# Narrow half first in some weight units, early parts for the fourth sums, a smaller first load and three more warm-up matmuls

## Chip, cores and metric

The kernel runs on one core of a Trainium2 chip. The metric is the device time of one execution in microseconds (us), the median of several runs. Engines are TensorE (PE; PEld is its weight load), VectorE (DVE), ScalarE (ACT), GpSimd (POOL) and SyncE (SP, which only issues DMAs here).

## What is computed

One layer of a streaming encoder on x of 512 tokens by 2048 channels, all in float32:

```
hn    = rmsnorm(x, norm_g)
proj  = hn @ w_in           # 3 branches x (q, k, v, gate) x 512, 4 forget logits, 3 x 2048 merge gates
ya    = forgetting_attention(...)   # branch A, 4 heads of 128
yb    = chunked_relpos_attention(...)  # branch B
yc    = stick_breaking_attention(...)  # branch C
ys    = stack(ya, yb, yc) * silu(gate)
merged = sum over branches of sigmoid(merge gates) * (ys @ w_up)
out   = x + merged @ w_out
```

q and k of branches A and B are normed per head. The three big products (with w_in, w_up and w_out) are nearly all of TensorE's work.

## The kernel before

**Operands in two parts.** Every float32 operand of a big product is split into a high part (rounded by a ScalarE copy, line 245) and a low part (the rest, a VectorE subtraction, line 249); a product is high x high, high x low and low x high. For weights the tiles are wh and wl. For the moving side a Parts tile holds high and low of 256 tokens side by side, so one matmul of 512 columns does high weights times both parts (wide), and one of 256 columns does low weights times the high part (narrow).

**Fewer products.** Two neighbouring column tiles of 128 are computed together in a PairTask by seven products instead of eight, over halves of the channels and of the tokens (the Strassen scheme). Products 1, 2, 3 and 5 read quarters of x (or of merged, the m tiles) or sums of them, products 6 and 7 read the tiles t23 (m23), product 4 reads t4 (m4): the "fourth sums". Each product is one weight unit of eight 128x128 tiles, a Pair: eight wide matmuls, then eight narrow ones (`mms_of`, lines 646 to 680). In most tasks the order is 1, 2, 6, 5, 7, 3, 4, and products 6, 7, 4 and 3 add onto the PSUM bank of an earlier one (`onto`). A `late` task and the very last product are all narrow (`single`): 24 matmuls of 256 columns. VectorE makes the weight sums for products 6 and 3 (`sums`, lines 625 to 639); those for 7 and 5 come by a second, adding DMA.

**Stages.** First a quad of four column tiles over the 16 channel tiles, in nine spans as x arrives (`first_quad`); then one late task and 45 other tasks on x, with the attention's small matmuls put between them; then the up-projection, where each of 16 output tiles has two units of 18 wide matmuls (three branches), whose results are weighted by gates reloaded from DRAM and added (`taken`); then eight tasks with w_out on the merged tiles, the first of them late.

**The merged tiles.** When output tiles k and k+8 are there, `merged_b` (lines 1399 to 1430) splits one of them, makes the sums of the two, and waits for room: `up_half` and `up_done` are set when the up-projection's last unit begins and when the first unit of the output projection begins, and free operand tiles (xps). The parts of product 4's sums, m4, are made last, in `late_t4` (lines 1432 to 1441): the unsplit sums wait in working tiles mu, two to a tile.

**What sets the order.** A planner, `Flow`, runs the whole program as tasks with costs per operation and due times, and writes the orders of TensorE, ScalarE and VectorE by hand; a task's spawn gives its slack, which sets its due time. `stream` (line 1529) walks the units on TensorE; `prep` splits a unit's weights, spawned two units ahead, with three buffers each for wh and wl. Working tiles of 512 columns (t2) are 20 in number, one of which holds constants (onef, zerof, nu_f) for good; raw weights have six (raws). Loads go on SP's queue, the first weights on ScalarE's, adding DMAs on POOL's.

**The start.** One DMA, `begin`, brings the first tile of x and all small constants (lines 292 to 299). VectorE copies two of them (gq, w2) ahead of its first work on x. POOL fills constants; `onef` is the third. Sixteen matmuls of constants (WARM, line 1543) run first on TensorE.

Of the kernel before, what the change touches and what calls it, by code (L numbers as in the profile page):

```python
# [15 lines left out]
P = 128  # L16
# [46 lines left out]
class Flow:  # L63
# [98 lines left out]
def hybrid_kernel(  # L162
# [2 lines left out]
    xT: bass.AP,  # L165
    xn: bass.AP,
    begin: bass.AP,
    w_one: bass.AP,
    w_two: bass.AP,
    w_col: bass.AP,  # L170
# [28 lines left out]
    def t2(s, dt=F32):  # L199
        return tp.tile([P, S], dt, tag="t2", name=nm(s))  # L200
# [14 lines left out]
    def blk(i):  # L215
        return slice(i * P, (i + 1) * P)
# [46 lines left out]
    def mm(ps, w, x, start=False, stop=False, more=False):  # L263
        nc.tensor.matmul(ps, w, x, start=start, stop=stop, skip_group_check=more)  # L264
# [30 lines left out]
    gn = small_in[:, 0:KT]  # L295
    gqk = small_in[:, KT:KT + 4]
    bfc = small_in[:, KT + 4:KT + 5]
    bg = small_in[:, KT + 5:KT + 5 + NB * DT]
    wf = small_in[:, KT + 5 + NB * DT:].rearrange("p (k h) -> p k h", h=NH)

    epsc = cp.tile([P, 1], F32, name="epsc")
    nc.gpsimd.memset(epsc, EPS)
    nhepsc = cp.tile([P, 1], F32, name="nhepsc")
    nc.gpsimd.memset(nhepsc, -0.5 * EPS)
    tmpc = t2("tmpc")
    onef, zerof, nu_f = tmpc[:, blk(0)], tmpc[:, blk(1)], tmpc[:, blk(2)]
    nc.gpsimd.memset(onef, 1.0)
# [20 lines left out]
    nc.gpsimd.memset(zeroc, 0.0)  # L328

    gq = cp.tile([P, 4], F32, name="gq")  # L330
    nc.vector.tensor_copy(gq, gqk)
    for c in (0, 2):
        nc.vector.tensor_scalar_mul(gq[:, c:c + 1], gqk[:, c:c + 1], SCALE)  # L333

    w2 = cp.tile([P, KT * NH + 32], F32, name="w2")
    nc.vector.tensor_copy(w2[:, :KT * NH].rearrange("p (k h) -> p k h", k=KT), wf)
    nc.vector.tensor_copy(w2[:, KT * NH:], zerof[:, :32])
    t2s.free.pop()


# [11 lines left out]
    class Unit:  # L352


        def __init__(self, mms, after=None, shape=(UK, P), srcs=()):
            self.shape, self.mms, self.after, self.srcs = list(shape), mms, after, srcs
            self.ready_hi, self.ready, self.there, self.raw = Event(), Event(), Event(), None

        def source_there(self):
            return self.there  # L360
# [208 lines left out]
    class Pair(Unit):  # L569


        def __init__(self, task, i):
            super().__init__(task.mms_of(i), task.after_of(i))
            self.task, self.p = task, task.order[i]

        def source_there(self):
            if self is self.task.units[0]:
                spawn(self.task.sums(), 3.0)
            return self.task.there[self.p]

        def source(self):
# [6 lines left out]
    class PairTask:  # L588
# [57 lines left out]
        def mms_of(self, i):  # L646
            p = self.order[i]
            bank = (0, 1, 2, 0, 0, 1, 2)[i] if self.late else {2: 1, 5: 2, 3: 2}.get(p, 0)
            onto = None if self.late else {6: 1, 7: 6, 4: 7, 3: 5}.get(p)
            more = onto is not None  # L650
            single = self.late or self.plain_end and p == 4
            self.bank = getattr(self, "bank", {})
            self.bank[p] = bank

            def go(u):
                if more:
# [6 lines left out]
                for j in range(UK):  # L663
                    yield lambda: self.ops[p](j) is not None
                    r, _, ev = self.ops[p](j)
                    yield ev
                    if single:
                        yield PE, mm_us(HS)
                        mm(self.ps[p][:, LH], u.hi[:, j, :], r[:, 0, :], j == 0 and not more, more=more)
                    else:  # L670
                        yield PE, mm_us(S)
                        mm(two(self.ps[p]), u.hi[:, j, :], r, j == 0 and not more, more=more)
                    if single:
                        yield PE, mm_us(HS)
                        mm(self.ps[p][:, LH], u.hi[:, j, :], r[:, 1, :], more=more)
                yield u.ready
                for j in range(UK):
                    yield PE, mm_us(HS)
                    mm(self.ps[p][:, LH], u.lo[:, j, :], self.ops[p](j)[1], stop=j == UK - 1, more=more)
            return go  # L680

        def after_of(self, i):
# [701 lines left out]

        return [Unit(mms(i), shape=(6, P), srcs=[w_up[d, i]]) for i in range(2)]

    m1, m2, m23, m4 = [None] * UK, [None] * UK, [None] * UK, [None] * (UK // 2)
    m4_ev = [Event() for _ in range(UK // 2)]
    kept_m, m1_ev, mus, up_half, up_done = {}, [Event() for _ in range(UK)], {}, Event(), Event()

    def merged_a(k, a):

# [6 lines left out]
    def merged_b(k, b):  # L1399
        a = kept_m[k]  # L1400
        yield m1_ev[k]
        yield t2s, 1
        t = t2("mt")
        if k % 2 == 0:
            yield t2s, 1
            mus[k // 2] = t2("mu")
        u = mus[k // 2][:, RH if k % 2 else LH]
# [24 lines left out]
    def late_t4(k, u, due):  # L1432
        if k % 2 == 0:
            yield xps, 1
            m4[k // 2] = Parts("m4")
            set_(m4_ev[k // 2])
        yield m4_ev[k // 2]
        h, lo, ev = m4[k // 2].half(k % 2)
        yield from split(h, lo, u, HS, ev, (due + 14.0,))
        if k % 2:  # L1440
            give(t2s)

    for k in range(UK):
        for d in (k, k + UK):
# [4 lines left out]
    at(len(units), freed(xps, 6, up_done))  # L1449


    mops = strassen_ops(m1, m2, m23, m4)

    def out_pair(e):
        evs = [Event(), Event()]
# [42 lines left out]
    def loads():  # L1498
        def x(kt):
            if kt == 0:  # L1500
                xraw[kt], x_in[kt].t = x_begin, landing(0.0, 256)
                return
            yield t2s, 1
            xraw[kt] = t2("x")
            x_in[kt].t = fetch(xraw[kt], xT[kt], 0.0, 256).t

        def n(i):
            yield t2s, 1
            t = t2("xn")
            n_in[i].t = fetch(t, xn[i // NQ, i % NQ], 0.0, 256).t  # L1510
            spawn(square_x(i, t), 10.0)

        todo = list(range(NQ * QB))
        for i, sp in enumerate(spans):

            for kt in [kt for sp in spans[i:i + (2 if i > 2 else 1)] for kt in range(*sp)]:
                if xraw[kt] is None:
                    yield from x(kt)
            yield from load_unit(units[i])
            if i >= N_FROM:  # L1520
                for _ in range(N_PER):
                    if todo:
                        yield from n(todo.pop(0))
        for i in todo:
            yield from n(i)
        for u in units[len(spans):]:
            yield from load_unit(u)

    def stream():
        for i, u in enumerate(units):  # L1530
            cur[0] = i
            for g in side.pop(i, ()):
                spawn(g(), 5.0, flow.fin)
# [3 lines left out]
            yield u.ready_hi  # L1537
            yield from u.mms(u)
            if u.after is not None:
                spawn(u.after(), 0.0, flow.fin)  # L1540
# [16 lines left out]

NT = 20
KEPT = 1
WARM = 16  # L1560
SPANS = [(0, 1), (1, 2)] + [(k + h, k + h + 2) for k in range(0, UK, 2) for h in (0, UK)][1:]
N_ONE = 2
NX = 28
# [56 lines left out]
```

## Time and profile before

| | us |
|---|---|
| median of three timed runs | 1327.93 |
| the three runs | 1326.29, 1327.93, 1328.51 |
| the profiled execution's own time | 1328.65 |
| its span, first to last instruction | 1326.9 |
| TensorE busy in the span | 1320.2 |
| VectorE busy | 1134.7 |
| ScalarE busy | 805.9 |

The span is what the trace shows; the execution's own time has the little before and after it. In a timeline row stand the start and the time taken in us, the engine, the line, the operation, out<-in by the program's names, the shape, the count of instructions merged in the row, and in brackets the idle time before it with what ended it. Matmuls overlap: a row's time taken holds the tail of its last one, so the pace is read from start to start. A wide matmul shows as 128x512, a narrow one as 128x256; a row with wh uses the high weights, one with wl the low ones.

### The profile page before, as it was taken

The numbers are of one execution on the slowest core, as the hardware profiler recorded it, in microseconds if no ns is written. First come the engines' busy times: TensorE is split into PE (matmuls) and PEld (weight loads), VectorE is DVE, ScalarE is ACT, GpSimd is POOL, SyncE is SP. The second block draws the span as 40 slices with busy tenths as digits, with TensorE's granted clock in tenths as the row PEclk, the third lists the DMA queues.
The fourth block names the chain that finished last, engine by engine and source line by source line (L and its number), as shares of the span: only waits on it lengthen the run. The fifth ranks groups of instructions, "written<-read, shape, count | busy, mean of one in ns | idle before, by whom it ended". The sixth has DMA issues, their size and how long they took to land.

```text
span 1326.9 us, 20238 instructions
## 1 busy us (share of the span) xinstructions
PE 1320.2 (99%) x7506; PEld 1150.5 (87%) x7506; DVE 1134.7 (86%) x1676; ACT 805.9 (61%) x1280; POOL 94.9 (7%) x120
## 2 busy tenths in 40 slices
PE   9999999999999999999999999999999999999998
PEld 6898888888888888888888888888888888888887
DVE  8989888788888889888898979888898877897786
ACT  8767657575556665666656665666557655454443
POOL 0000001000010100000000000000000000001000
PEclk9999999999999999999999999999999999999999
DMA  9776776767786776867878777776779755668893
GB/s 336 207 206 168 190 198 176 212 177 190 200 203 172 197 201 181 219 160 207 200 182 215 173 193 201 192 196 181 194 178 272 278 194 184 193 172 243 235 254 94
DMA packets 89651, 266.24 MB, mean 201 GB/s; under 512 B 10560, under 2 KB 12608, under 8 KB 89552
## 3 DMA queue, kind: packets, MB, share of 16 engines
q1 hardware_dynamic: 70400, 203.86, 46.4%
q0 software_dynamic: 15552, 56.63, 25.8%
q10 hardware_dynamic: 3600, 4.46, 0.9%
q8 instruction: 59, 0.97, 0.3%
q14 instruction: 40, 0.33, 0.1%
HBM read 245.21 MB, written 19.70 MB: 200 GB/s over the span
## 4 chain that ended last, share of the span: by engine, by line
PE 98%; DVE 1%; DMA 0%; issue 0%; DVEq 0%
PE acc L264 84%; PE att L264 8%; PE att L1008 1%; PE att L259 1%; PE att L260 1%; PE att L1121 1%; PE att L1122 1%; PE att L261 1%; PE att L1120 1%; PE att L1072 0%; PE att L1222 0%; DMA begin_in<-in_begin 0%; PE att L909 0%; PE att L910 0%; DVE m L249 0%; DVE wl L249 0%
## 5 line engine op out<-in xcount | busy, mean ns | idle before, releaser
L249 DVE TENSOR_TENSOR wl<-raw,wh 128x1024 fp32r<-128x1024 f32 (+2 forms) x418 | 499.8, 1199 | 141.9 <-ACT wh L245 133.6
L245 ACT ACTIVATE wh<-raw 128x1024 fp32r<-128x1024 f32 (+2 forms) x418 | 434.1, 1039 | 145.3 <-PE acc L264 62.3
L264 PE MATMUL acc<-x,wh 128*128 128x512 f32 (+1 forms) x1568 | 399.2, 391 | 0.7 <-DVE gq L333 0.7
L264 PEld LDWEIGHTS acc<-x,wh 128*128 128x128 f32 x1568 | 277.3, 189 | 50.1 <-issue 2.2
L264 PE MATMUL acc<-t,wh 128*128 128x512 f32 (+1 forms) x1128 | 283.7, 390 | 0.0
L264 PEld LDWEIGHTS acc<-t,wh 128*128 128x128 f32 x1128 | 198.1, 189 | 32.9
L264 PEld LDWEIGHTS acc<-x,wl 128*128 128x128 f32 x1504 | 207.0, 190 | 17.2 <-DVE x L441 0.8
L264 PE MATMUL acc<-x,wl 128*128 128x256 f32 (+1 forms) x1504 | 216.8, 285 | 0.0
L264 PEld LDWEIGHTS acc<-t,wl 128*128 128x128 f32 x1104 | 151.6, 190 | 11.4
L264 PE MATMUL acc<-t,wl 128*128 128x256 f32 x1104 | 155.5, 282 | 0.0
L282 POOL DMA_DIRECT2D raw<-in_w_col x92 | 79.5, 864 | 924.1 <-DMA raw<-in_w_col 573.8
L264 PE MATMUL acc<-m,wh 128*128 128x512 f32 (+1 forms) x512 | 113.7, 366 | 1.5 <-DVE m L249 1.5
L264 PEld LDWEIGHTS acc<-m,wh 128*128 128x128 f32 x512 | 85.4, 190 | 14.4 <-DVE m L249 1.9
L815 ACT ACTIVATE c<-acc 128x256 f32<-128x256 f32 x51 | 19.6, 383 | 97.1 <-PE acc L264 94.1
L782 ACT ACTIVATE u<-acc 128x512 f32<-128x512 f32 x51 | 30.3, 594 | 79.4 <-PE acc L264 79.4
L761 ACT ACTIVATE u<-acc 128x512 f32<-128x512 f32 x52 | 31.1, 598 | 71.9 <-PE acc L264 70.8
L637 DVE TENSOR_TENSOR raw<-raw,raw 128x1024 f32<-128x1024 f32 x54 | 65.9, 1220 | 0.5
L631 DVE TENSOR_TENSOR raw<-raw,raw 128x1024 f32<-128x1024 f32 x54 | 65.8, 1219 | 0.4
L264 PE MATMUL att<-y,wh 128*128 128x512 f32 x256 | 65.8, 389 | 0.0
L264 PEld LDWEIGHTS acc<-m,wl 128*128 128x128 f32 x448 | 60.6, 191 | 3.7
L264 PE MATMUL acc<-m,wl 128*128 128x256 f32 x448 | 62.5, 282 | 0.0
L264 PEld LDWEIGHTS att<-y,wh 128*128 128x128 f32 x256 | 48.0, 188 | 10.0
(207 smaller groups left out, 1397.2 us busy)
## 6 DMA issues: line engine op xcount, KB each, us to landing
raw<-in_w_col SPq DMA_DIRECT2D x230, 512.0 KB, 4.5
raw<-in_w_col POOLq DMA_DIRECT2D x92, 512.0 KB, 6.4
raw<-in_w_out SPq DMA_DIRECT2D x40, 512.0 KB, 5.3
gl<-c SPq DMA_DIRECT2D x48, 256.0 KB, 3.5
raw<-in_w_up SPq DMA_DIRECT2D x32, 384.0 KB, 3.6
sg<-gl SPq DMA_DIRECT2D x48, 256.0 KB, 4.8
raw<-in_w_out POOLq DMA_DIRECT2D x16, 512.0 KB, 6.9
xn<-in_xn SPq DMA_DIRECT2D x16, 256.0 KB, 3.1
```

The source lines that it names most:

```text
L245: nc.scalar.activation(hi, src, AF.Copy)
L249: nc.vector.tensor_sub(lo, src, f(hi))
L259: nc.tensor.matmul(ps, lh, rh, start=start, stop=False, skip_group_check=more)
L260: nc.tensor.matmul(ps, lh, rl, start=False, stop=False, skip_group_check=more)
L261: nc.tensor.matmul(ps, ll, rh, start=False, stop=stop, skip_group_check=more)
L264: nc.tensor.matmul(ps, w, x, start=start, stop=stop, skip_group_check=more)
L282: nc.gpsimd.dma_start(to, src, accum_op=ALU.add)
L631: nc.vector.tensor_add(w[1], w[1], w[5])
L637: nc.vector.tensor_add(w[2], w[2], w[1])
L761: nc.scalar.activation(self.u, ps, AF.Copy)
L782: nc.scalar.activation(self.s, ps, AF.Copy)
L815: nc.scalar.activation(c, ps[:, RH], AF.Copy, scale=-1.0)
```

## The change

Five edits.

1. **Turned units.** A Pair that is not all narrow may run its narrow half first. `stream` decides it for each unit when it comes up: the unit before ended with its narrow half, this one adds onto a bank that is already begun (products 6, 7, 4 and 3), and the planner has its low weights ready at least AHEAD = 0.4 us before. A turned unit ends wide, so the next one is not turned. It waits for its low weights at its start.
2. **Plain sums** are spawned with a slack of 1.5 instead of 3.0.
3. **Early fourth sums.** `late_t4` is gone; `merged_b` makes the sums in place in b's right half and splits them at once into a working tile of their own, m4, which is kept to the end. Six instead of five of the m23 wait only for `up_half`.
4. **First load.** Only norm_g comes with x's first tile. The other constants have a load of their own, issued on ScalarE's queue behind the first unit's weights; the small copies from them (gq, w2) become a task for VectorE from 9 us on.
5. **Warm-ups.** POOL fills onef first; 19 instead of 16 matmuls of constants.

```diff
-    x_begin, small_in = begin_in[:, :S], begin_in[:, S:]
+    small_in = cp.tile([P, consts.shape[1]], F32, name="small_in")
+    x_begin, gn = begin_in[:, :S], begin_in[:, S:]
...
+    tmpc = t2("tmpc")
+    onef, zerof, nu_f = tmpc[:, blk(0)], tmpc[:, blk(1)], tmpc[:, blk(2)]
+    nc.gpsimd.memset(onef, 1.0)
     epsc = cp.tile([P, 1], F32, name="epsc")
...
+    def small_parts():
+        yield DVE, 0.8
+        nc.vector.tensor_copy(w2[:, :KT * NH].rearrange("p (k h) -> p k h", k=KT), wf)
+        nc.vector.tensor_copy(gq, gqk)
+        for c in (0, 2):
+            nc.vector.tensor_scalar_mul(gq[:, c:c + 1], gqk[:, c:c + 1], SCALE)
...
+            self.single = task.late or task.plain_end and self.p == 4
+            self.onto = None if task.late else {6: 1, 7: 6, 4: 7, 3: 5}.get(self.p)
...
-                spawn(self.task.sums(), 3.0)
+                spawn(self.task.sums(), 1.5)
...
+                def low(first):
+                    yield u.ready
+                    for j in range(UK):
+                        yield lambda: self.ops[p](j) is not None
+                        _, x, ev = self.ops[p](j)
+                        yield ev
+                        yield PE, mm_us(HS)
+                        mm(self.ps[p][:, LH], u.lo[:, j, :], x, first and j == 0 and not more,
+                           not first and j == UK - 1, more)
+
+                steps = (low, high) if u.low_first else (high, low)
+                for first, step in zip((True, False), steps):
+                    yield from step(first)
...
         yield q
-        minus(u, t[:, LH], b[:, LH])
+        minus(b[:, RH], t[:, LH], b[:, LH])
+        yield t2s, 1
+        parts, ev = t2("m4", F32R), Event()
+        yield from split(parts[:, LH], parts[:, RH], b[:, RH], HS, ev)
         give(t2s)
-        ready = up_half if k < 5 else up_done
+        m4[k] = two(parts), parts[:, LH], ev
+        ready = up_half if k < 6 else up_done
...
-        yield up_done
-        yield from late_t4(k, u, due)
...
+            if i == 0:
+                nc.scalar.dma_start(small_in, consts)
...
             yield u.ready_hi
+            if isinstance(u, Pair) and not u.single:
+                low_there = u.ready.t is not None and u.ready.t + AHEAD <= flow.clock[PE]
+                u.low_first = ends_low and u.onto is not None and low_there
+                ends_low = not u.low_first
+            else:
+                ends_low = False
             yield from u.mms(u)
...
+    spawn(small_parts(), 2.0, 9.0)
...
+AHEAD = 0.4
+WARM = 19
```

`high` is the wide half's loop as it was, now a function beside `low`.

More of the change, by code (lines that the diff above doesn't have):

```diff
@@ L167, in hybrid_kernel @@
     begin: bass.AP,
+    consts: bass.AP,
     w_one: bass.AP,
@@ L292, in hybrid_kernel @@
     begin_in = cp.tile([P, begin.shape[1]], F32, name="begin_in")
-    x_begin, small_in = begin_in[:, :S], begin_in[:, S:]
+    small_in = cp.tile([P, consts.shape[1]], F32, name="small_in")
+    x_begin, gn = begin_in[:, :S], begin_in[:, S:]
     first = [tc.keep_in_program_order(nc.sync.dma_start(begin_in, begin))]
[L295 to L299, printed above, removed]
+    gqk = small_in[:, 0:4]
+    bfc = small_in[:, 4:5]
+    bg = small_in[:, 5:5 + NB * DT]
+    wf = small_in[:, 5 + NB * DT:].rearrange("p (k h) -> p k h", h=NH)
+    tmpc = t2("tmpc")
+    onef, zerof, nu_f = tmpc[:, blk(0)], tmpc[:, blk(1)], tmpc[:, blk(2)]
+    nc.gpsimd.memset(onef, 1.0)
     epsc = cp.tile([P, 1], F32, name="epsc")
@@ L304, in hybrid_kernel @@
     nc.gpsimd.memset(nhepsc, -0.5 * EPS)
-    tmpc = t2("tmpc")
-    onef, zerof, nu_f = tmpc[:, blk(0)], tmpc[:, blk(1)], tmpc[:, blk(2)]
-    nc.gpsimd.memset(onef, 1.0)
     nc.gpsimd.memset(zerof, 0.0)
@@ L357, in __init__ @@
             self.ready_hi, self.ready, self.there, self.raw = Event(), Event(), Event(), None
+            self.low_first = False
         def source_there(self):
@@ L648, in mms_of @@
             bank = (0, 1, 2, 0, 0, 1, 2)[i] if self.late else {2: 1, 5: 2, 3: 2}.get(p, 0)
-            onto = None if self.late else {6: 1, 7: 6, 4: 7, 3: 5}.get(p)
-            more = onto is not None
-            single = self.late or self.plain_end and p == 4
             self.bank = getattr(self, "bank", {})
@@ L655, in go @@
             def go(u):
+                single, onto = u.single, u.onto
+                more = onto is not None
                 if more:
@@ L661, in go @@
                     self.ps[p] = acc(bank)
[L663 to L667, printed above, removed]
-                        yield PE, mm_us(HS)
[L669 to L679, printed above, removed]
+                def high(first):
+                    for j in range(UK):
+                        yield lambda: self.ops[p](j) is not None
+                        r, _, ev = self.ops[p](j)
+                        yield ev
+                        start, stop = first and j == 0 and not more, not first and j == UK - 1
+                        if single:
+                            yield PE, mm_us(HS)
+                            mm(self.ps[p][:, LH], u.hi[:, j, :], r[:, 0, :], start, stop, more)
+                            yield PE, mm_us(HS)
+                            mm(self.ps[p][:, LH], u.hi[:, j, :], r[:, 1, :], more=more)
+                        else:
+                            yield PE, mm_us(S)
+                            mm(two(self.ps[p]), u.hi[:, j, :], r, start, stop, more)
@@ new lines, in low @@
+                def low(first):
+                    yield u.ready
+                    for j in range(UK):
+                        yield lambda: self.ops[p](j) is not None
+                        _, x, ev = self.ops[p](j)
+                        yield ev
+                        yield PE, mm_us(HS)
+                        mm(self.ps[p][:, LH], u.lo[:, j, :], x, first and j == 0 and not more,
+                           not first and j == UK - 1, more)
+                steps = (low, high) if u.low_first else (high, low)
@@ L1385, in up_units @@
         return [Unit(mms(i), shape=(6, P), srcs=[w_up[d, i]]) for i in range(2)]
-    m1, m2, m23, m4 = [None] * UK, [None] * UK, [None] * UK, [None] * (UK // 2)
-    m4_ev = [Event() for _ in range(UK // 2)]
-    kept_m, m1_ev, mus, up_half, up_done = {}, [Event() for _ in range(UK)], {}, Event(), Event()
+    m1, m2, m23, m4 = [None] * UK, [None] * UK, [None] * UK, [None] * UK
+    kept_m, m1_ev, up_half, up_done = {}, [Event() for _ in range(UK)], Event(), Event()
     def merged_a(k, a):
@@ L1403, in merged_b @@
         t = t2("mt")
[L1404 to L1407, printed above, removed]
         q = DVE, dve_us(HS)
@@ L1428, in merged_b @@
         give(t2s)
-        yield up_done
-        yield from late_t4(k, u, due)
[L1432 to L1441, printed above, removed]
     for k in range(UK):
@@ L1449, in hybrid_kernel @@
     at(len(units), freed(xps, 6, up_done))
-    mops = strassen_ops(m1, m2, m23, m4)
+    mops = strassen_ops(m1, m2, m23, None)
+    mops[4] = lambda k: m4[k]
     def out_pair(e):
@@ L1537, in stream @@
             yield u.ready_hi
+            if isinstance(u, Pair) and not u.single:
+                low_there = u.ready.t is not None and u.ready.t + AHEAD <= flow.clock[PE]
+                u.low_first = ends_low and u.onto is not None and low_there
+                ends_low = not u.low_first
+            else:
+                ends_low = False
             yield from u.mms(u)
@@ L1600 @@
         "xn": g["x"][0].reshape(QB, P, DT // NQ, S).transpose(0, 2, 1, 3),
-        "begin": np.concatenate([xT[0]] + consts, axis=1),
+        "begin": np.concatenate([xT[0], consts[0]], axis=1),
+        "consts": np.concatenate(consts[1:], axis=1),
         "w_one": np.stack([first(*sp) for sp in SPANS[:N_ONE]]),
```

5 lines of the change are left out of this document (removed).

## Prediction

> **What bounds the kernel now.** I read the page first: the busy times and the shares of the chain.
>
> ```profile
> span 1326.9 us, 20238 instructions
> PE 1320.2 (99%) x7506; PEld 1150.5 (87%) x7506; DVE 1134.7 (86%) x1676; ACT 805.9 (61%) x1280; POOL 94.9 (7%) x120
> PE 98%; DVE 1%; DMA 0%; issue 0%; DVEq 0%
> ```
>
> TensorE is the chain. Nothing hides a change on it, so a gain must be fewer idle TensorE microseconds or less time per matmul. The second reading is therefore the spacing of its starts, in TensorE's own timeline: a weight unit in the steady part, then the chain where every matmul is 512 wide.
>
> ```profile
> 124.53 2.00 PE L264 MATMUL acc<-x,wh 128*128 128x512 f32 x8
> 126.37 1.12 PE L264 MATMUL acc<-x,wl 128*128 128x256 f32 x8
> ...
> 138.50 0.86 PE L264 MATMUL acc<-x,wh 128*128 128x512 f32 x3
> ```
> ```profile
> 1036.18 5.44 PE att L264 x24
> ...
> 1044.34 5.44 PE att L264 x24
> ```
>
> Five units take 138.50 - 124.53 = 13.97 us, 2.794 each: eight wide matmuls (high weights), then eight narrow ones (low weights). In the chain, 36 wide ones in a row take 1044.34 - 1036.18 = 8.16 us, 0.2267 each. The third reading is the first task of the output projection, where all matmuls are narrow.
>
> ```profile
> 1163.86 2.08 PE L264 MATMUL acc<-m,wh 128*128 128x256 f32 x16
> ...
> 1181.13 1.08 PE L264 MATMUL acc<-m,wh 128*128 128x256 f32 x7
> 1182.38 0.84 PE L264 MATMUL acc<-m,wh 128*128 128x256 f32 x4 [0.16 <-DVE m L249]
> 1184.52 1.05 PE L264 MATMUL acc<-m,wh 128*128 128x256 f32 x5 [1.30 <-DVE m L249]
> ...
> 1186.36 2.00 PE L264 MATMUL acc<-m,wh 128*128 128x512 f32 x8
> ```
>
> Six units of 24 narrow matmuls take 1181.13 - 1163.86 = 17.27 us, 0.1199 each. So sixteen matmuls that did not mix would take 8 x 0.2267 + 8 x 0.1199 = 2.773 us, where a unit takes 2.794. Going wide, narrow, wide costs 0.021 us per unit. The seventh unit, from 1181.13, should take 24 x 0.1199 = 2.88 us and takes 5.23: TensorE loses 2.35 us waiting for VectorE's m tiles. The fourth reading is the first ten microseconds.
>
> ```profile
> 0.80 0.10 POOL L302 MEMSET epsc<- 128x1 f32 x1 [0.29 <-POOLq L1611]
> 0.87 0.20 POOL L307 MEMSET tmpc<- 128x128 f32 x1
> 1.13 3.60 PE L1544 MATMUL att<-tmpc 128*128 128x256 bf16 x16 [1.13 <-POOL tmpc L307]
> 4.61 0.17 DVE L331 COPY gq<-begin_in 128x4 f32<-128x4 f32 x1 [2.04 <-DMA begin_in<-in_begin]
> 4.79 0.72 ACT L390 ACTIVATE wh<-raw 128x256 fp32r<-128x256 f32 x2 [2.71 <-DMA raw<-in_w_one]
> 4.79 0.48 DVE L435 TENSOR_SCALAR x<-begin_in 128x512 fp32r<-128x512 f32 x1
> 5.42 1.19 PE L264 MATMUL acc<-x,wh 128*128 128x512 f32 x2 [0.69 <-DVE gq L333]
> 7.26 1.05 PE L264 MATMUL acc<-x,wh 128*128 128x512 f32 x2
> 8.11 1.05 PE L264 MATMUL att<-x,wh 128*128 128x512 f32 x2
> 9.66 1.06 ACT L245 ACTIVATE wh<-raw 128x1024 fp32r<-128x1024 f32 x1
> 9.82 0.68 PE L264 MATMUL att<-x,wl 128*128 128x512 f32 x2
> 10.34 0.62 PE L264 MATMUL acc<-x,wh 128*128 128x512 f32 x2
> ```
>
> Until 9.82 two wide matmuls take 8.11 - 7.26 = 0.85 us, twice the later 0.45: half pace. The first unit's twelve matmuls take 10.34 - 5.42 = 4.92 us where 12 x 0.2267 = 2.72 would do. 2.2 us go there, and the gap before 5.42 belongs to it.
>
> **The change, term by term.** The profiled execution took 1328.65 us (span 1326.9); the median of the three timed runs is 1327.93, 0.72 lower. I add my terms to 1328.65.
>
> *First data.* The first load shrinks from 16+4+1+48+64 constants beside x to 16: 2580 to 2112 bytes per partition, 58.5 KB less.
>
> ```profile
> GB/s 336 207 206 168 190 198 176 212 177 190 200 203 172 197 201 181 219 160 207 200 182 215 173 193 201 192 196 181 194 178 272 278 194 184 193 172 243 235 254 94
> ```
>
> At the first slice's 336 GB/s that is 0.17 us, for x and for the weights that land beside it (ScalarE's 4.79). VectorE's two copies before x (4.61 to 4.79) also go behind the prep of x. Without them x starts near 4.44 and ends near 4.92; the first half of the weights (half of 0.72) ends near 4.98. First matmul about 5.13 instead of 5.42: **-0.29** (bounds 0 and -0.42). The constants' own load is queued behind the first weights on ScalarE's queue, where the first work on data is that 4.79; nobody needs them before the small matmuls of the forget gate, two weight units later, and the late copies (each like the 0.17 us of gq) lie beside TensorE's work of those units. Without that cover they cost what they cost now, nothing more.
>
> *Pace at the start.* With onef filled first, warm-ups begin at about 1.06; sixteen end near 1.13 + 16 x 0.213 = 4.54 (256 columns at half pace, 0.85 / 4), leaving 0.88 us empty. Nineteen end near 5.11: no gap. In the trace 3.4 us of warm-ups followed by the gap did not raise the pace; 4.4 us of unbroken matmuls (5.42 to 9.82) did. Unbroken from 1.06, the pace should rise between 4.5 and 5.5 if that is the count, and at worst at 9.5. The bounds are thus -2.2 and 0; I take **-1.7**, near the first. The Trainium skill, "TensorE: Matmul & The Clock Gate", Part 1, says that the window is a free-running 3.41 us, so the rise may come anywhere from one to two windows after the first warm-up. By that rule (an estimate from the page) the middle is at 6.2 us and the term -1.7 as well, with a spread between runs that no single trace shows.
>
> TensorE then comes 2 us earlier to everything behind. The second double unit's weights end at 9.66 + 1.06 = 10.72 and would be wanted at 5.13 + 2 x 2.72 = 10.6 at best.
>
> ```profile
> 53.78 2.01 ACT L245 ACTIVATE wh<-raw 128x1024 fp32r<-128x1024 f32 x2 [0.58 <-DMA raw<-in_w_col]
> ...
> 56.99 2.08 PE L264 MATMUL acc<-x,wh 128*128 128x256 f32 x16
> ```
>
> The weights of the first task after the quad end at 54.8 behind a DMA; wanted at 56.99, then at 55.0. Both covers are used up: **+0.2** (0 to 0.6).
>
> *Turned units.* In a task's order 1, 2, 6, 5, 7, 3, 4 the units 6, 7 and 4 follow one that ended narrow, and may run their narrow half first. Each saves one full change of width, 0.021 us. There are 45 such tasks on x and 7 on m, 3 units each, without the last plain unit: 155, so at most 3.3 us. What may forbid it: the low weights must be there 1.84 us sooner, at the unit's start. The tightest two kinds in the trace:
>
> ```profile
> 899.10 1.22 DVE L249 TENSOR_TENSOR wl<-raw,wh 128x1024 fp32r<-128x1024 f32 x1
> ...
> 900.56 0.63 PE L264 MATMUL acc<-t,wh 128*128 128x512 f32 x2
> ```
> ```profile
> 379.36 1.22 DVE L249 TENSOR_TENSOR wl<-raw,wh 128x1024 fp32r<-128x1024 f32 x1
> ...
> 381.05 0.63 PE L264 MATMUL acc<-t,wh 128*128 128x512 f32 x2
> ```
>
> The first is 0.24 us ahead (four units are like it), the second 0.47 (fourteen); all others have more. The planner turns a unit only with 0.4 us in its own account, so these 18 may stay. About 146 x 0.021 = **-3.1** (bounds 0 and -3.3). A turned unit holds its high weights' buffer longer, by the eight narrow matmuls (0.96 us); the third unit after it gets that buffer, and should its split come too late for its own turn, that is the slower rival below. If the change of width only moved elsewhere, the term would be nothing. "TensorE: Matmul & The Clock Gate" of the Trainium skill, Back-to-back issue gap, gives a gap from a matmul's own width alone; by it order cannot matter and the term is 0, which is a rival below. The rows above (2.794 against 2.773) differ from it.
>
> *Early fourth sums.* VectorE now makes the fourth sums' parts while the up-projection runs, one per merge, instead of after it.
>
> ```profile
> 1179.97 0.75 DVE L249 TENSOR_TENSOR m<-mu,m 128x256 fp32r<-128x256 f32 x2
> ...
> 1181.24 0.42 DVE L249 TENSOR_TENSOR m<-mu,m 128x256 fp32r<-128x256 f32 x1
> ...
> 1181.91 0.75 DVE L249 TENSOR_TENSOR m<-mu,m 128x256 fp32r<-128x256 f32 x2
> ...
> 1184.05 1.09 DVE L249 TENSOR_TENSOR m<-mu,m 128x256 fp32r<-128x256 f32 x3
> ```
>
> All eight stand between 1180 and 1185, just where TensorE waits 2.35 us; done early, that wait goes. What is late next is the 6th and 7th sums:
>
> ```profile
> 1175.37 2.08 PE L264 MATMUL acc<-m,wh 128*128 128x256 f32 x16
> 1176.30 0.68 DVE L249 TENSOR_TENSOR m<-mt,m 128x512 fp32r<-128x512 f32 x1
> ```
>
> The eighth of these ends at 1176.98, wanted at 1175.37 + 14 x 0.12 = 1177.05: no slack. One or two early splits of 0.38 us may now stand ahead of it. So **-2.0** (bounds -2.35 and -1.2). The fourth parts hold eight of the 19 working tiles to the end where four were held before.
>
> The earlier due time of the plain sums (1.5 for 3.0) moves VectorE work only: 0. Sum: -0.29 - 1.7 + 0.2 - 3.1 - 2.0 = -6.9. **1328.65 - 6.9 = 1321.8 us**, 0.46% under the median.
>
> **The rivals.**
> *The pace does not rise earlier* (the gap stays, or the count starts at the first data): 1.7 is lost, 1323.5. For it: the weights' first half may come late and leave a hole. 0.13.
> *Turning brings nothing*: the excess belongs to each unit's own first wide matmuls, not to the change of width. Then 1321.8 + 3.1 = 1324.9. Against it: the wide groups from 1036.18 on start new weights too, at 0.2267. 0.07.
> *Working tiles run short*: eight fourth parts and up to eight kept sums of the 6th and 7th leave three to five of 19 when the last gate values load.
>
> ```profile
> sg<-gl SPq DMA_DIRECT2D x48, 256.0 KB, 4.8
> ```
>
> Gates are asked for three half-units, 12.2 us, ahead and need 4.8 + 0.7 us; a whole half-group (8.16 us) late, TensorE waits some 1.5 us, and ScalarE and VectorE start the output late, taking the 2.0 back: 1325.3. 0.09.
> *Slower: low weights come late at turned units.* VectorE is 86% busy, and its lateness, hidden by the 1.84 us of wide matmuls, would become TensorE's idle time. It needs about 1 us of slip at the 18 tight units if these are turned (18 x 0.55 = 10 us): 1332. It decides from a slip of some 0.5 us past the slack; against it, the trace shows no TensorE wait on low weights, and the 0.4 us margin. 0.07.
>
> **How the numbers follow.** My case has 0.64, its own range 1320.4 to 1323.9. A measurement tells 0.2% (2.7 us) from no change, so faster means under 1325.3, slower over 1330.6. Faster: 0.64, 0.13 and half of the two middle rivals, 0.85; same 0.08; slower 0.07. The range reaches from all terms at their best (-8.3, and some of the 0.7 between profiled run and median) to the short tiles: 1320.0 to 1325.4.
>
> **What would show it.** Right: rows of sixteen narrow, then sixteen wide matmuls where a turned unit stands; first data near 5.1 with full pace well before 9.8; no wait on m near 1181. Wrong: TensorE waiting for wl at a unit's start, spacing after sixteen narrow ones above 0.24, waits between 1150 and 1180.

## The result and the profile after

The changed kernel takes 1322.18 us in the median of six runs (1321.85 to 1322.86); the kernel before takes 1327.76 in its six runs on the same chip (1326.29 to 1328.51). The ratio is 0.996, 95% interval 0.9948 to 0.9972: 5.6 us less, where 1321.8 was forecast. The profiled execution took 1322.19 us, 6.46 less than the profiled one before, which lies 0.9 us above the median of its kernel. The head of its page:

```profile
span 1320.5 us, 20303 instructions
PE 1315.7 (100%) x7509; PEld 1150.3 (87%) x7509; DVE 1133.9 (86%) x1676; ACT 809.7 (61%) x1280; POOL 95.1 (7%) x120
```

The span is 6.4 us shorter, VectorE and ScalarE are as busy as before: the work is the same, TensorE waits less and spaces its matmuls a little closer. To see where, I take the start of the same weight unit in both traces and subtract; the lead can grow only where something was won. (The differences are taken before rounding.)

| unit | before, us | after, us | lead, us | won since the row above |
|---|---|---|---|---|
| first data | 5.42 | 5.02 | 0.39 | 0.39 |
| second single unit of the quad | 10.34 | 8.19 | 2.15 | 1.76 |
| first late task | 56.99 | 54.80 | 2.18 | 0.03 |
| first task that may turn units | 78.02 | 75.83 | 2.18 | 0.00 |
| up-projection | 1033.27 | 1028.95 | 4.32 | 2.14 |
| output projection, first task | 1163.86 | 1159.51 | 4.35 | 0.03 |
| its second task | 1186.36 | 1180.35 | 6.01 | 1.66 |
| last unit | 1320.44 | 1314.07 | 6.37 | 0.36 |

The start, from the timeline of the changed kernel:

```profile
1.07 4.24 PE L1557 MATMUL att<-tmpc 128*128 128x256 bf16 x19 [1.07 <-POOL nhepsc L308]
...
4.37 0.49 DVE L440 TENSOR_SCALAR x<-begin_in 128x512 fp32r<-128x512 f32 x1 [1.78 <-DMA begin_in<-in_begin]
4.55 0.72 ACT L395 ACTIVATE wh<-raw 128x256 fp32r<-128x256 f32 x2 [2.47 <-DMA raw<-in_w_one]
...
5.02 1.05 PE L265 MATMUL acc<-x,wh 128*128 128x512 f32 x2
5.91 0.62 PE L265 MATMUL att<-x,wh 128*128 128x512 f32 x2
6.37 0.62 PE L265 MATMUL acc<-x,wh 128*128 128x512 f32 x2
...
8.88 1.06 ACT L246 ACTIVATE wh<-raw 128x1024 fp32r<-128x1024 f32 x1
...
10.91 0.61 PE L265 MATMUL acc<-x,wh 128*128 128x512 f32 x2
```

x lands at 4.37 and work on it starts at once; the first data matmul follows at 5.02, right behind the warm-ups, and from 5.91 on two wide matmuls take 0.46 us (6.37 - 5.91), full pace. Before, that came after 9.82. The second double unit's weights end at 9.94, wanted at 10.91: no wait.

The output projection, TensorE's timeline:

```profile
1180.35 2.00 PE L265 MATMUL acc<-m,wh 128*128 128x512 f32 x8
1182.19 1.11 PE L265 MATMUL acc<-m,wl 128*128 128x256 f32 x8
1183.14 2.00 PE L265 MATMUL acc<-m,wh 128*128 128x512 f32 x8
1184.98 2.08 PE L265 MATMUL acc<-m,wl 128*128 128x256 f32 x16
1186.89 3.82 PE L265 MATMUL acc<-m,wh 128*128 128x512 f32 x16
1190.55 2.08 PE L265 MATMUL acc<-m,wl 128*128 128x256 f32 x16
1192.46 3.82 PE L265 MATMUL acc<-m,wh 128*128 128x512 f32 x16
```

Rows of sixteen are the turned units: the narrow half of one unit and of the next, then two wide halves. Sixteen wide ones take 1190.55 - 1186.89 = 3.66 us, where two separate eights take 2 x 1.84. 134 units are turned: 39 of product 6, 44 of 7, 43 of 4 and 8 of 3.

The first output task, where TensorE lost 2.35 us:

```profile
1171.14 1.96 PE L265 MATMUL acc<-m,wh 128*128 128x256 f32 x15
1173.42 0.38 PE L265 MATMUL acc<-m,wh 128*128 128x256 f32 x1 [0.32 <-DVE m L250]
...
1177.46 2.08 PE L265 MATMUL acc<-m,wh 128*128 128x256 f32 x16
1179.38 1.12 PE L265 MATMUL acc<-m,wl 128*128 128x256 f32 x8
1180.35 2.00 PE L265 MATMUL acc<-m,wh 128*128 128x512 f32 x8
```

The last unit (product 4, from 1177.46) now takes 2.89 us without a hole. In its place the unit of product 6 loses 0.5 us (1173.42 - 1171.14 - 15 x 0.12) ahead of its last matmul with high weights, waiting for the last of the m23 parts.

### The profile page after: what moved, and what is told of

Same layout as the page of the kernel before. It is cut to its first block, busy times and chain, and to the rows that moved or that the text cites. A ratio compares the mean times of both kernels' runs of the same rounds, so it can differ in the third digit from the quotient of the medians.

```text
span 1320.5 us, 20303 instructions
## 1 busy us (share of the span) xinstructions
PE 1315.7 (100%) x7509; PEld 1150.3 (87%) x7509; DVE 1133.9 (86%) x1676; ACT 809.7 (61%) x1280; POOL 95.1 (7%) x120
## 4 chain that ended last, share of the span: by engine, by line
PE 99%; DVE 0%; ACT 0%; issue 0%; POOL 0%; ACTq 0%; POOLq 0%
PE acc L265 85%; PE att L265 8%; PE att L1025 1%; PE att L260 1%; PE att L261 1%; PE att L1138 1%; PE att L1139 1%; PE att L262 1%; PE att L1137 1%; PE att L1089 0%; PE att L1557 0%; PE att L1239 0%; PE att L926 0%; PE att L927 0%; DVE m L250 0%; DVE wl L250 0%
## 5 line engine op out<-in xcount | busy, mean ns | idle before, releaser
L265 PEld LDWEIGHTS acc<-x,wh 128*128 128x128 f32 x1568 | 283.5, 189 | 55.1 <-issue 2.2
L265 PE MATMUL acc<-t,wh 128*128 128x512 f32 (+1 forms) x1128 | 280.0, 388 | 0.0
L265 PEld LDWEIGHTS acc<-t,wl 128*128 128x128 f32 x1104 | 144.8, 191 | 1.9
L265 PE MATMUL acc<-m,wh 128*128 128x512 f32 (+1 forms) x512 | 109.6, 364 | 0.3 <-DVE m L250 0.3
L265 PE MATMUL acc<-m,wl 128*128 128x256 f32 x448 | 59.8, 283 | 0.0
```

## The experiments

All twelve kernels were timed beside the kernel before on the same chip, whose medians there were 1328.36 (first four), 1328.34 (next four), 1328.26 (next three) and 1327.97 (last). Its executions lie in two groups, near 1326.8 and near 1328.5, so its median moves with their shares; its shortest ones agree (1326.3 to 1326.7 in all sets), and I compare the medians of single-group kernels directly with 1322.18.

### 1. No unit turned

```diff
-AHEAD = 0.4
+AHEAD = 1e9
```

> The changed kernel with no unit turned (every unit wide half first), all else kept. My theory, a change of width costs TensorE 0.021 us and 134 turned units save one each: 134 x 0.019 to 0.021 = 2.5 to 2.8 us more, 1324.7 to 1325.0. Rival, the spacing depends on a matmul's own width alone and the 2.5 us between the stages come from other shifts in the order: 1322.2 as with turning.

Measured: 1325.03 us (1324.5 to 1325.52), 2.85 more than the changed kernel. In the two profiled executions the distance to the changed kernel grows by 2.05 us between the first task and the up-projection (from -0.11 to 1.93) and by 0.36 from the second output task on, close to the table above. Turning is worth 2.3 to 2.9 us; the spacing does depend on the neighbour.

### 2. Sixteen warm-ups

```diff
-WARM = 19
+WARM = 16
```

> The changed kernel with 16 warm-up matmuls for 19; the hole before the first data is about 0.55 us wide, for 0.88 before. My theory, unbroken activity from the first warm-up on raises the pace: with the hole the rise comes some 3 to 4 us later and costs 1 to 2 us, 1323.2 to 1324.2. Rival, the earlier first data and the earlier fill alone did it, the hole does not matter: 1322.2.

Measured: 1324.31 us; the five runs lie in two groups, 1322.10 and 1322.46, 1324.31 to 1324.54. The profiled one is of the upper group:

```profile
1.06 3.59 PE L1557 MATMUL att<-tmpc 128*128 128x256 bf16 x16 [1.06 <-POOL nhepsc L308]
5.46 1.22 PE L265 MATMUL acc<-x,wh 128*128 128x512 f32 x2 [0.80 <-ACT wh L395]
6.48 1.05 PE L265 MATMUL att<-x,wh 128*128 128x512 f32 x2
...
9.89 0.67 PE L265 MATMUL att<-x,wl 128*128 128x512 f32 x2
```

With the hole (0.80 us) the pace is half until 9.89, as before the change. But not in each execution: two runs are as short as with nineteen. The hole makes the late pace possible, not certain.

### 3. Fourth sums late again

```diff
-        minus(b[:, RH], t[:, LH], b[:, LH])
-        yield t2s, 1
-        parts, ev = t2("m4", F32R), Event()
-        yield from split(parts[:, LH], parts[:, RH], b[:, RH], HS, ev)
+        minus(u, t[:, LH], b[:, LH])
...
-        ready = up_half if k < 6 else up_done
+        ready = up_half if k < 5 else up_done
...
+        yield up_done
+        yield from late_t4(k, u, due)
```

> The changed kernel with the fourth sums split after the up-projection, as before the change. My theory, VectorE's eight late splits are what TensorE waited for: the wait near the end of the first output task is back and the time is 1.6 to 2.0 us longer, 1323.8 to 1324.2. Rival, the wait came from VectorE's load as a whole in that stage and moves with any order: 1322.2 to 1322.9.

Measured: 1323.70 us (1323.48 to 1325.26), 1.5 more. The wait is back at the old place:

```profile
1176.78 1.85 PE L265 MATMUL acc<-m,wh 128*128 128x256 f32 x11
1179.94 1.06 PE L265 MATMUL acc<-m,wh 128*128 128x256 f32 x5 [1.30 <-DVE m L250]
```

### 4. Wide and narrow one by one

```diff
-                u.low_first = ends_low and u.onto is not None and low_there
+                u.mix = low_there
...
+                if u.mix:
+                    yield from mixed()     # for each j: the wide matmul, then the narrow one
```

> The changed kernel, but instead of turning, each unit whose low weights are there in time runs wide and narrow matmuls in turn, one by one (eight changes from narrow to wide in a unit). If every single change from narrow to wide costs 0.021 us: some 340 units x 7 more changes = 50 us more, near 1375. If the cost is only what the first five wide matmuls pay after a run of narrow ones, and one narrow matmul between two wide ones costs no more than its width: units of 2.77 us, some 340 x 0.021 = 7.1 us less than with no turned unit, near 1317.7.

Measured: 1327.58 us (1327.17 to 1327.89, and one at 1331.02 with a granted clock of 0.949), 2.55 more than with no unit turned; neither number. 317 units ran mixed:

```profile
130.28 0.28 PE L265 MATMUL acc<-t,wl 128*128 128x256 f32 x1
130.40 0.39 PE L265 MATMUL acc<-t,wh 128*128 128x512 f32 x1
130.63 0.28 PE L265 MATMUL acc<-t,wl 128*128 128x256 f32 x1
130.75 0.39 PE L265 MATMUL acc<-t,wh 128*128 128x512 f32 x1
```

A pair takes 0.35 us (130.63 - 130.28). In a plain unit, by the single starts in the trace before, the eight wide matmuls take 233, 236, 228, 232, 231, 227, 227, 227 ns and the narrow ones 113, 119, then 120. So the first five wide ones pay some 6, 10, 2, 5 and 4 ns, and 7 and 1 ns come back in the first two narrow ones: 27 less 8, about 0.02 us in a unit. One by one, a wide matmul takes 233 ns on x and a narrow one 117: 2.80 us in a unit, 0.005 more than plain. On m the wide one takes 237: 2.83 us, 0.033 more. The profiled executions, 3.36 us apart, show it: beside experiment 1 the mixed kernel loses 1.2 us in the 274 units on x and 1.4 in the 43 on m; another 0.75 lies at the start, where the pace rose later (6.8 for 5.0). So a change does not cost the same everywhere, not even in the same place after it. What in TensorE does this no run tells.

### 5. The old first load

```diff
-    x_begin, gn = begin_in[:, :S], begin_in[:, S:]
+    x_begin, gn, small_in = begin_in[:, :S], begin_in[:, S:S + KT], begin_in[:, S + KT:]
...
+    nc.vector.tensor_copy(gq, gqk)
...
+    nc.vector.tensor_copy(w2[:, :KT * NH].rearrange("p (k h) -> p k h", k=KT), wf)
```

> The changed kernel with the first load and the small copies as before (all constants beside x's first tile, the four copies ahead of the work on it); onef first and 19 warm-ups stay. My theory, less bytes and no copies gave the 0.39 us of earlier first data: first data at 5.3 to 5.4 again, a hole of 0.3 us behind the warm-ups, 1322.4 to 1322.8, and up to 2 us more in executions where even that hole delays the pace. Rival, first data come when the weights land, whatever lies beside x: 1322.2, first data near 5.0.

Measured: 1322.77 us (1322.66 to 1324.80), 0.6 more.

```profile
4.69 0.17 DVE L333 COPY gq<-begin_in 128x4 f32<-128x4 f32 x1 [2.10 <-DMA begin_in<-in_begin]
4.76 0.19 DVE L336 COPY w<-begin_in 128x64 f32<-128x64 f32 x1
4.87 0.48 DVE L436 TENSOR_SCALAR x<-begin_in 128x512 fp32r<-128x512 f32 x1
...
5.49 0.94 PE L264 MATMUL acc<-x,wh 128*128 128x512 f32 x2 [0.19 <-DVE gq L335]
6.28 0.63 PE L264 MATMUL att<-x,wh 128*128 128x512 f32 x2
```

x lands 0.32 us later (4.69 for 4.37), work on it starts 0.5 later, and first data are at 5.49. The pace rises early even so, and four of five runs pay the delay alone. But the landing itself differs as much between executions: x lands at 4.37 to 4.93 us in the ten traces with the small load and at 4.54 to 4.96 in the four with the old one, so an effect of the bytes does not show. What is steady is the time from there to the first data matmul, 0.64 to 0.73 us in the ten and 0.80 to 0.81 in the four: the copies cost 0.15. What makes the rest of the 0.6 us in the median stays open.

### 6. No warm-ups

```diff
-WARM = 19
+WARM = 0
```

> The changed kernel without any warm-up matmul. Count theory, some 4.4 us of unbroken matmuls raise the pace: rise near 9.5, 1324.2 to 1324.6 in all executions. Free-running window of 3.4 us: rise anywhere from 8.4 to 11.9, executions spread over 1.7 us, median near 1324.8. Rival, warm-ups do not matter: 1322.2.

Measured: 1324.30 us (1323.41 to 1324.86), 2.1 more, spread over 1.45 us. In the profiled one the pace rises at 10.2, 4.96 us after the first matmul at 5.25.

### 7. No margin for turning

```diff
-AHEAD = 0.4
+AHEAD = 0.0
```

> The changed kernel with no margin asked of the low weights (AHEAD 0.0 for 0.4), so that more units are turned, some 150 for 134. If the low weights are on the chip when the planner says, each further turned unit saves 0.02 us: 1321.8 to 1322.0. Rival, the slower case of the prediction, VectorE is late at the tight units: TensorE waits there for wl, 0.1 to 0.5 us at each of some 15 units, 1323.5 or more.

Measured: 1322.22 us (1322.21 to 1322.40). Only two more units turn, 136, so this does not put the slower rival to the test: the other units are not ready by the planner's account at all. The tight units of the prediction were not tried turned.

### 8. Product 4 ahead of 6 and 7

```diff
             self.order = (1, 5, 2, 3, 6, 7, 4) if late else (1, 2, 6, 5, 7, 3, 4)
+            if late and rest is not None:
+                self.order = (1, 5, 2, 3, 4, 6, 7)
```

> The changed kernel with product 4 ahead of products 6 and 7 in the first output task (order 1, 5, 2, 3, 4, 6, 7). My theory, the 0.7 us that TensorE still waits there is for the parts of the 6th and 7th sums, which stand behind all others on VectorE, while the fourth parts are there long before: with 2.9 us more the wait goes, 1321.5. Rival, VectorE is short in that stage whatever the order, and the wait only moves: 1322.2.

Measured: 1323.41 us, 1.2 more. The wait in the first output task is gone (it takes 20.27 us, 20.84 in the changed kernel), but the last task now waits for its weights' parts:

```profile
1303.98 2.10 PE L265 MATMUL acc<-m,wh 128*128 128x512 f32 x8 [0.70 <-ACT wh L246]
1306.48 1.22 PE L265 MATMUL acc<-m,wl 128*128 128x256 f32 x8 [0.40 <-DVE wl L250]
```

Parts of the 6th and 7th sums were what TensorE waited for, as held; the planner's other order gives 1.5 us back some 120 us later, so the 1321.5 us expected were missed.

### 9. The start alone

The kernel before with edits 4 and 5 (small load, late copies, onef first, nineteen warm-ups).

```diff
-    x_begin, small_in = begin_in[:, :S], begin_in[:, S:]
+    x_begin, gn = begin_in[:, :S], begin_in[:, S:]
...
+                nc.scalar.dma_start(small_in, consts)
...
-WARM = 16
+WARM = 19
```

> The kernel before with the start's edits alone (small first load, late copies, onef first, 19 warm-ups). My theory: first data 0.39 us earlier and the pace up before 8 us in every execution. The kernel before has executions near 1326.7 and near 1328.6; the first group is one whose pace rose early, so this one should have a single group 0.4 to 0.6 us under the first: 1326.0 to 1326.4. Rival, the two groups have another cause: two groups again, each 0.4 lower, median near 1328.0.

Measured: 1327.79 us (1326.29 to 1328.58), only 0.5 under the kernel before (ratio 0.9997, 0.9988 to 1.0006: not to be told from no change); a miss, and the most useful one. In its profile the lead is 2.26 us from the first tasks to the output projection, all that the start should give. Then TensorE's timeline and the windows' view (TensorE, its weight loads, VectorE, ScalarE and POOL busy; then the granted clock, the DMA share and GB/s) show:

```profile
1180.12 0.84 PE L265 MATMUL acc<-m,wh 128*128 128x256 f32 x4 [0.16 <-DVE m L250]
1182.26 1.34 PE L265 MATMUL acc<-m,wh 128*128 128x256 f32 x5 [1.30 <-DVE m L250]
1183.40 1.91 PE L265 MATMUL acc<-m,wl 128*128 128x256 f32 x8
1185.11 2.38 PE L265 MATMUL acc<-m,wh 128*128 128x512 f32 x8
...
1188.27 2.00 PE L265 MATMUL acc<-m,wh 128*128 128x512 f32 x8
```
```profile
1176.00:1180.00 4.00, 3.96 (x33) 3.73 (x31) 3.97 (x10) 0.72 (x2) 0.86 (x1) 1.00 0.79 180
1180.00:1184.00 4.00, 2.58 (x12) 2.32 (x13) 4.00 (x9) 0.63 (x1) 0.00 (x0) 0.81 0.92 221
1184.00:1188.00 4.00, 4.00 (x21) 3.57 (x20) 4.00 (x6) 1.06 (x1) 0.86 (x1) 0.76 0.52 114
```

The granted clock falls to half for about 3.4 us (4 x 0.19 x 2 + 4 x 0.24 x 2; the trace's own clock record has it from 1182.50 to 1185.91) behind the wait for the fourth sums: eight narrow matmuls take 1.71 us (1185.11 - 1183.40) for 0.95. From 1182.26 to the next task's first unit it is 2.85 us, where the kernel before takes 1186.36 - 1184.52 = 1.84, and that unit takes 1188.27 - 1185.11 = 3.16 for 2.79. So 1.4 of the 2.26 us are given back. The wait costs its own length and, in some executions, the pace after it. The mean granted clock of each timed execution fits: 3.41 us at half lower it by 0.0013, and it is 0.999 in the eight longest of the eleven and 1.0 in the three shortest (1326.29, 1326.52, 1327.02). In experiment 3, which has the same wait, only the long execution (1325.26) reads 0.999. The reading is no proof alone, as two of the changed kernel's six have it and are not longer; nor is it shown why the kernel before, with the same wait, has it in only 2 of its 22 executions there.

### 10. Turning alone

The kernel before with edits 1 and 2; load, fourth sums and warm-ups as before.

```diff
+                low_there = u.ready.t is not None and u.ready.t + AHEAD <= flow.clock[PE]
+                u.low_first = ends_low and u.onto is not None and low_there
```

> The kernel before with the turned units alone (and the sums' slack of 1.5); start and fourth sums as before. If the terms add up: 2.5 to 2.8 us under the kernel before on the same chip, and its two groups as before, 1325.6 to 1325.9 in the median. Rival, turning pays only with the other edits (VectorE free at the end, earlier start): under 1.5 us.

Measured: 1325.88 us, 2.4 under the kernel before; the runs in two groups, 1323.64 to 1324.19 and 1325.85 to 1326.32, 2 us apart as in that kernel. Turning pays by itself.

### 11. Earlier due time for the parts of the 6th and 7th sums

```diff
-        yield from split(m23[k].hi, m23[k].lo, two(t), S, ev, (due + 7.0,))
+        yield from split(m23[k].hi, m23[k].lo, two(t), S, ev, (due + 3.5,))
```

> The changed kernel with the parts of the 6th and 7th sums due 3.5 us earlier (3.5 for 7.0 in their split). If the remaining 0.7 us wait in the first output task is a matter of order on VectorE, it goes without a new one and the time is 0.5 to 0.7 us less, 1321.5 to 1321.7. Rival, any other order there brings a wait elsewhere, as when product 4 was moved: 1322.2 or more.

Measured: 1324.13 us, 1.95 more. Now the low weights come behind those parts:

```profile
1171.87 1.21 PE L265 MATMUL acc<-m,wl 128*128 128x256 f32 x8 [1.42 <-DVE wl L250]
...
1175.41 0.39 PE L265 MATMUL acc<-m,wh 128*128 128x256 f32 x1 [0.53 <-DVE m L250]
```

VectorE is short in that stage; another order only chooses who waits. None of the twelve beats the changed kernel.

### 12. Early fourth sums alone

The kernel before with edit 3.

```diff
+        parts, ev = t2("m4", F32R), Event()
+        yield from split(parts[:, LH], parts[:, RH], b[:, RH], HS, ev)
...
-        ready = up_half if k < 5 else up_done
+        ready = up_half if k < 6 else up_done
```

> The kernel before with the early fourth sums alone; no unit turned, start as before. Term of the prediction: the wait of 2.35 us shrinks to 0.7, so 1.7 us less, 1326.3 to 1326.7 in the median. In one profiled execution of the start's edits alone the pace also fell to half for 3.4 us at that wait. If the wait does so in many executions of the kernel before, taking it away is worth more: 2.3 to 3 us, 1325.3 to 1326.0, and the executions lie closer together than those of the kernel before; if their spread comes from the start's hole alone, two groups 2 us apart remain.

Measured: 1326.45 us; eight runs at 1326.13 to 1326.60, three at 1328.31 to 1328.57. The first output task takes 20.85 us for 22.50, as it should. But the last tasks wait, as in experiment 8:

```profile
1306.03 2.11 PE L264 MATMUL acc<-m,wh 128*128 128x512 f32 x8 [0.44 <-ACT wh L245]
1308.54 1.21 PE L264 MATMUL acc<-m,wl 128*128 128x256 f32 x8 [0.40 <-DVE wl L249]
```

ScalarE's timeline shows what the weights stood behind:

```profile
1303.10 0.34 ACTq L1486 DMA_DIRECT2D out<-c  x1
1303.49 0.60 ACT L774 ACTIVATE u<-acc 128x512 f32<-128x512 f32 x1 [2.50 <-DVE c L1484]
1303.98 2.94 ACT L245 ACTIVATE wh<-raw 128x1024 fp32r<-128x1024 f32 x3
```

The store of a result waits for VectorE, and three splits of weights queue behind it. This takes 1.36 of the 1.65 us back. In experiment 1, which has the same early sums, the same unturned units, the new start and the plain sums' slack of 1.5, no such wait stands; that the slack is what matters is an inference, since the start differs too.
In the profile the pace rises at 4.1, still in the warm-ups, and the hole that follows does not lower it:

```profile
1.13 3.33 PE L1551 MATMUL att<-tmpc 128*128 128x256 bf16 x16 [1.13 <-POOL tmpc L306]
5.34 0.70 PE L264 MATMUL acc<-x,wh 128*128 128x512 f32 x2 [0.88 <-DVE gq L335]
5.88 0.62 PE L264 MATMUL att<-x,wh 128*128 128x512 f32 x2
```

So the two groups of the kernels with the start's hole are an early and a late pace: the same sixteen warm-ups and the same hole, full pace from 5.88 in one execution and from 9.8 in another. The groups that remained with edit 3 alone answer the question put: the kernel before owes them, in the main, to the start. No kernel has a profile of both groups, so this is put together from the traces of several.

## Why the prediction was right

*First data*, -0.29 forecast, -0.39 measured between these two executions; that they are near is luck. Of the 0.39 us, 0.24 are x landing earlier (4.37 for 4.61), which is inside the scatter of the landing with either load (experiment 5): the 0.17 reckoned for the bytes is not shown. The copies' part, 0.12 in the forecast, is, with 0.15.

*Pace*, -1.7 forecast, -1.76 measured between the first data and the second unit. Experiments 2 and 6 take it back. Of the two ways of reckoning, the count (a rise some 4.4 us after unbroken matmuls begin) fell: with the warm-ups in place the rise came from 2.9 us (experiment 7, at 4.0) to 5.7 us (experiment 4, at 6.8) after the first matmul. By the Trainium skill ("TensorE: Matmul & The Clock Gate", Part 1) the window runs free, whenever a kernel starts. The traces agree: the rise lies elsewhere in each, and in experiment 9 it is 1177.60 us from the rise at 4.90 to the fall at 1182.50, 345 times the 3.413 us of the half pace there. So the closeness of the number is luck too: the nine traces with nineteen warm-ups have the rise anywhere from 4.0 to 6.8. And the term holds only against executions whose pace rose late; the shorter group of the kernel before, if its pace rose early as in experiment 12, has little of it to win.

*The covers*, +0.2 forecast, 0 measured: the lead is 2.18 us from the second double unit to the first task. This step was wrong in kind. I held the weights' times fixed and moved TensorE towards them; they came earlier as well. At the second double unit it is 8.88 for 9.66, and this goes with the new first load and its order: 8.88 to 9.30 in the ten traces with the small load, the late pace of experiment 2 included (9.19), and 9.36 to 9.66 in the four with the old one. At the late task it goes with the pace:

```profile
51.90 2.01 ACT L246 ACTIVATE wh<-raw 128x1024 fp32r<-128x1024 f32 x2 [0.89 <-DMA raw<-in_w_col]
```

That is 51.90 for 53.78, 1.9 of TensorE's 2.2 us; the ten traces with an early rise have it at 51.42 to 52.86, the four with a late one at 53.15 to 54.17.

*Turning*, -3.1 forecast, -2.50 measured (2.14 on x, 0.36 on m). The cost of a change was right: 0.36 us for 18 turned units on m is 0.020 each, 2.14 for 116 on x is 0.018. The number was mis-sized: 146 units reckoned, 134 turned. The reckoning left out half of the 18 tight units; by the planner's account 21 were not ready (13 of product 6, 8 of product 7). Behind those 8 the unit of product 3 turned, which the forecast did not have, and so that of product 4 could not. The rival that only a matmul's own width counts fell with experiments 1 and 10. The slower rival did not show: no wait for wl at a turned unit stands in the trace of the changed kernel; the tight units were not turned, so what they would cost stays open.

*Fourth sums*, -2.0 forecast, -1.66 measured. What was said to be late next, the last part for product 6, is what waits now (0.5 of the 0.7 us left). This is the wait between 1150 and 1180 that was named as a sign of being wrong; it came, but at 0.5 us it stays inside the term's bounds. Experiment 12 shows that the term was not its own: with the plain sums' old slack and the old start it nets 0.3 us in the profile. The slack of 1.5, set at 0, may be worth more than nothing; experiments 12 and 1 differ in it and in the start.

*What the sum left out*: the wait for the fourth sums can halve the pace for a window. I charged it at its length. In the profiled execution of experiment 9 it cost 1.4 us more, and the start's edits alone gain only 0.5 us in the median. In the changed kernel, where that wait is 0.5 us, their 2.2 us stay. The parts measured alone give 0.5 + 2.4 + 1.5 = 4.4 us in medians (of kernels with two groups, so to about 1 us); together they give 5.6. The short working tiles, the third rival, did not show in the changed kernel.

The sum stands: 0.39 + 1.76 + 0.03 + 2.14 + 0.03 + 1.66 + 0.36 = 6.37 of 6.9 forecast from the profiled execution. The mechanisms of the large terms were right; that the sum came so near is in part luck, since turning and the fourth sums gave 0.9 us too little while the covers and the first data gave 0.3 more than reckoned.

## What to carry to other kernels

Where one engine is busy all the time, read the spacing of its starts in a stage where nothing is mixed and compare: here 0.021 us for each change of matmul width, 2.5 us over the kernel, could be read off before any run. A wait on TensorE is to be charged with what it does to the pace behind it, and edits that each take away a hole may be worth more together than one by one. A fixed order of instructions that is made anew at each edit may give a gain back far from the edit: follow the lead from stage to stage before calling a term its own.

## What the runs showed of the hardware that was not expected

The pace goes by windows of 3.413 us on a raster that does not start with the kernel. The half pace of experiment 9 lasts 3.413 us; from rise to fall it is 345 times that there, 386 times in the kernel before (1317.545 us) and 385 in the changed one (1314.131); and the rise lies at another time in each trace. I counted the idle time between matmuls in each such window, a matmul taken at its usual spacing (0.12 us for a narrow one at full pace). Windows with up to 0.49 us idle (experiments 5 and 12) raised it, those with 1.04 us (the kernel before, ahead of the one that raised it), 1.17 (experiment 2) and 1.38 us (experiment 10) did not. Once up, it stayed through windows with 1.7 us idle (the kernel before, to 1184) and fell after one with 2.2 us (experiment 9, the one trace with such a fall before the end). No single gap was longer than 1.5 us there, so a long pause is not needed to lose the pace.

A change of width costs by place in a plain unit, 6, 10, 2, 5 and 4 ns in the first five 512-wide matmuls after 256-wide ones, and it does not grow with the run of narrow ones: after 168 in a row (the first output task of the changed kernel) the wide ones take 233, 236, 228, 233 and 231 ns like those after eight.
